# mLSTM stabiliser: the running maximum spread by transfers through HBM and masked on GpSimd, in place of three products a head

## The chip, the cores and the metric

The kernel runs on one core of one Trainium2 chip. The metric is the device time of a run in microseconds (us), as the median of three runs. Five engines are spoken of: TensorE (PE, matrix products), VectorE (DVE), ScalarE (ACT), GpSimd (POOL) and SyncE (SP, which here issues most transfers). Each takes its own instructions strictly in order; they wait for one another by semaphores. PSUM is the memory that products accumulate in, SBUF the one that the engines work from.

## The reference

Two layers of a streaming-encoder trunk for 256 positions and a width of 1024, in float32. Each layer has a token mixer and a gated MLP. In the mixer one input projection feeds a latent attention (MLA, 8 heads) and an mLSTM (8 heads of 64), whose results are projected, merged by gates and projected again. A conditioning vector c gives shifts, scales and gates (adaLN) by a 1024 x 6144 projection per layer.

What the change touches is the mLSTM's stabiliser. In the reference, chunk by chunk:

```python
log_d = jnp.where(causal, b[..., :, None] - b[..., None, :] + ih[..., None, :], -jnp.inf)
log_inter = b + m[..., None]
m_t = jnp.maximum(log_inter, jnp.max(log_d, axis=-1))
w_intra = jnp.exp(log_d - m_t[..., None])
s = jnp.einsum("bthd,bshd->bhts", qc, kc) * w_intra
```

The kernel writes this over the whole sequence. With AA[s] the input gate less the summed log forget gates at position s, and M[t] the running maximum of AA (started at 0), the weight of source s for target t is exp(AA[s] - M[t]) for s <= t and 0 beyond. So each of the 8 heads needs its row M[t] on all 128 partitions (which hold s), and the triangle beyond the diagonal masked out.

## The kernel before

Activations lie transposed, channels on partitions, 256 positions along the free axis. Every float32 product is made of three products in a faster format: weights and activations are split in a high and a low part (`whi`, `wlo`, `hh`, `hl`), and whi x hh, whi x hl and wlo x hh are summed. A weight block of 128 x 1024 is loaded by SP (`raw`), rounded to `whi` by an ACT copy, and DVE subtracts to get `wlo`. DVE also works off the adaLN projection, blocks `ada` of 512 KB loaded by SP into two buffers, as a background task.

The order on the engines is that in which the program emits its instructions. The main line emits units of 4 slots, each with 12 weight products; side tasks (Python generators: heads, gates, norms) go on by one step a slot, at each of their `yield`s. In the mixer the main line runs "fillers", the weight products of other projections, and the heads of both branches run beside them as side tasks: `mlstm_head` and, some slots behind it, the attention head `mla_head`. After heads 1 and 3 no filler follows (PLAIN_HEADS), so heads 1 and 2 start in one slot, and 3 and 4. An attention head makes its scores (`kall`, `qall`), ACT exponentiates them (p), scales them by the inverse sum, PE transposes them (`cst`, the identity, with p), ACT copies them out, and PE multiplies by the values `vv`.

`gates` (line 689 on) makes AA and, by a scan on DVE (line 743), M as an 8 x 256 tile. Before the change ACT rounds M into `mr` rows 0 to 7 and DVE writes the remainder into rows 32 to 39. `mlstm_head` (line 881 on) spreads a row by products: a selector `selr` with ones in the two rows of a head gives M[t] on all partitions in a PSUM bank E (256 columns, then 128 again for the second half of s), and the identity times `maskr` adds the mask of large numbers to the two diagonal blocks. One slot later ACT takes exp(AA - E) from the bank into `dd`; one later DVE multiplies with the query-key products S (`qm`, `km`) to `pw`; one later PE multiplies `pw` with the values `vaug`. Every fourth head goes on with the output of four heads.

`late_constants` (line 1311 on), a side task in the first units, fetches the selector and the mask by two transfers issued on ACT's queue, and ten slots later copies them into `selr` and `maskr` on ACT. POOL adds squares for the norms, takes rsqrt by a power, and issues the transfers that spread the rotary key (`kr` to `kall`); its rows are else empty during the heads. Temporary tiles of one size share a ring of buffers (`w384`: 6 of 128 x 384 numbers), so a new tile waits for the last reader of the one that it takes over. DVE and ACT have a window of 8, so that an emission order differs little from the executed one.

Of the kernel before, what the change touches and what calls it, by code (L numbers as in the profile page):

```python
# [19 lines left out]
P = 128  # L20
T = 256
# [47 lines left out]
NATIVE = 2  # L69
DELAYS = dict(kr=6, c=1, gates=3)  # L70
MLA_DELAY = (3, 2)
LATER = (2, 2, 2, 1)


# [117 lines left out]
def hybrid_trunk(ctx, tc, a):  # L192
# [15 lines left out]
    upool = pool("upool", 1)  # L208
    work = pool("work", 1)
    psum = pool("psum", 1, PSUM)  # L210

    uid = [0]

    def nm(s):
        uid[0] += 1
        return f"{s}_{uid[0]}"

    def bank():
        return psum.tile([P, 512], F32, name=nm("bank"), tag="bank", bufs=8)
# [1 line left out]
    def w256(dt=F32, tag="w256", bufs=8):  # L221
        return work.tile([P, T], dt, name=nm(tag), tag=tag, bufs=bufs)

    def w384(tag="w384", bufs=6):
        return work.tile([P, 384], F32, name=nm(tag), tag=tag, bufs=bufs)

    def w512(tag="w512", bufs=4):
# [375 lines left out]
    def mixer(l, n, begun):  # L603
# [24 lines left out]
        stA, sA = sub("cqkv")  # L628
        gt = sA.tile([40, T], F32, name=nm("gt"), tag="gt")
        ats = sA.tile([8, T], F32, name=nm("ats"), tag="ats")  # L630
        M = sA.tile([8, T], F32, name=nm("M"), tag="M")
        cc_ = sA.tile([P, 5, T], F32, name=nm("cqkv"), tag="cqkv")
        cbank = bank()
        later = LATER if begun else (0,) * 4
# [54 lines left out]
        def gates():  # L689
            b1 = bank()  # L690
            for tb in range(2):
                pe.transpose(b1[:, tb * 40:tb * 40 + 40], gt[:, tb * P:(tb + 1) * P], ident[:40, :40])
            yield
            dve.tensor_copy(gs, b1[:, :80].rearrange("p (b g) -> p b g", b=2))
            iT, fT = gs[:, :, 0:8], gs[:, :, 32:40]

            def g8():
                return work.tile([P, 2, 8], F32, name=nm("g8"), tag="g8", bufs=10)

            ab = g8()  # L700
            dve.scalar_tensor_tensor(ab, fT, -1.0, fT, ALU.mult, ALU.max)
            e = g8()
            act.activation(e, ab, AF.Exp, scale=-1.0)
            yield
            r = g8()
            dve.tensor_scalar(r, e, 2.0, None, ALU.add)
            dve.reciprocal(r, r)
            u = g8()
            dve.tensor_tensor(u, e, r, ALU.mult)
            u2 = g8()  # L710
            dve.tensor_tensor(u2, u, u, ALU.mult)
            p = g8()
            dve.tensor_scalar(p, u2, 1.0 / 17.0, None, ALU.mult)
            for d in (15.0, 13.0, 11.0, 9.0, 7.0, 5.0, 3.0):
                dve.scalar_tensor_tensor(p, p, 1.0 / d, u2, ALU.add, ALU.mult)
            dve.scalar_tensor_tensor(p, p, 1.0, u, ALU.add, ALU.mult)
            mn = g8()
            dve.tensor_scalar(mn, fT, 0.0, None, ALU.min)
            lf = g8()
            dve.scalar_tensor_tensor(lf, p, -2.0, mn, ALU.mult, ALU.add)  # L720
            mg = 1.5 * 2.0 ** 15
            for src, dst in ((lf, LF), (iT, II)):
                dve.tensor_scalar(dst[:, :, 0:8], src, mg, -mg, ALU.add, ALU.add)
                dve.tensor_tensor(dst[:, :, 8:16], src, dst[:, :, 0:8], ALU.subtract)
            for _ in range(6 + later[0]):
                yield
            cs = bank()
            pe.matmul(cs[:, 0:16], tri, LF[:, 0, :], start=True, stop=True)
            pe.matmul(cs[:, 16:32], ones, LF[:, 0, :], start=True, stop=False)
            pe.matmul(cs[:, 16:32], tri, LF[:, 1, :], start=False, stop=True)  # L730
            yield
            dve.tensor_copy(CS, cs[:, 0:32].rearrange("p (b g) -> p b g", b=2))
            dve.tensor_tensor(AA, II, CS, ALU.subtract)
            act.activation(ealo, AA[:, :, 8:16], AF.Exp)
            for _ in range(2 + later[1]):
                yield
            dve.tensor_copy(vaug[:, :, :, 64], ealo)
            at = bank()
            for tb in range(2):
                pe.transpose(at[0:8, tb * P:(tb + 1) * P], AA[:, tb, 0:8], ident)  # L740
            yield
            dve.tensor_copy(ats, at[0:8, :T])
            dve.tensor_tensor_scan(M, ats, ats, 0.0, ALU.max, ALU.max)
            act.copy(mr[0:8], M)
            for _ in range(2 + later[2]):
                yield
            dve.tensor_tensor(mr[32:40], M, mr[0:8].bitcast(F32), ALU.subtract)
            mt_ = bank()
            for tb in range(2):
                pe.transpose(mt_[:, tb * 8:tb * 8 + 8], M[:, tb * P:(tb + 1) * P], ident[:8, :8])  # L750
            yield
            m = g8()
            dve.tensor_tensor(m, mt_[:, 0:16].rearrange("p (b g) -> p b g", b=2), CS[:, :, 0:8], ALU.add)
            dve.tensor_tensor(m, m, CS[:, :, 8:16], ALU.add)
            act.activation(floor, m, AF.Exp, scale=-1.0)
# [123 lines left out]
                                  ALU.subtract)  # L879

        def mlstm_head(hd, nb, spair):
            E = bank()
            sl = selr[:, hd:hd + 1].to_broadcast([40, P])
            pe.matmul(E[:, 0:T], sl, mr, start=True, stop=False)
            pe.matmul(E[:, T:384], sl, mr[:, P:T], start=False, stop=False)
            pe.matmul(v2(E)[:, :, 0:P], identr, maskr.unsqueeze(1).to_broadcast([P, 2, P]), start=False, stop=True)
            if not spair:
                for r0 in (0, 64):
                    spair.append((bank(), qm[hd // 4][r0:r0 + 64, hd // 2 % 2, :],
# [3 lines left out]
                for S, q_, k_ in spair:  # L893
                    pe.matmul(S[:, T:384], k_[:, P:T], q_[:, P:T], start=True, stop=True)
            S = spair[hd % 2][0]
            yield
            dd = w384()
            act.activation(dd[:, 0:T], E[:, 0:T], AF.Exp, scale=-1.0, bias=AA[:, 0, hd:hd + 1])
            act.activation(dd[:, T:384], E[:, T:384], AF.Exp, scale=-1.0, bias=AA[:, 1, hd:hd + 1])
            yield  # L900
            pw = w384()
            dve.scalar_tensor_tensor(pw, S[:, :384], 1.0 / 32.0, dd, ALU.mult, ALU.mult)
# [399 lines left out]
    W.queue_split(W.at)  # L1302
    W.flush()
    pe.window, act.window, dve.window, gp.window = 1000, 8, 8, 1000
    mr = const.tile([40, T], F32R, name="mr")
    gp.memset(mr.bitcast(F32), 0.0)
    selr = const.tile([40, NH], F32R, name="selr")
    identr = const.tile([P, P], F32R, name="identr")
    maskr = const.tile([P, P], F32R, name="maskr")

    def late_constants():
        for _ in range(8):
            yield
        act.copy(identr, ident)
        todo = ((selr, "sel", small(NH)[0:40]), (maskr, "mask", w256()[:, :P]))
        for _, src, t in todo:
            with tc.issue_after(act.done[-1]):
                nc.scalar.dma_start(t, a[src])
        for _ in range(10):
            yield  # L1320
        for dst, _, t in todo:
            act.copy(dst, t)

    setup_stack.close()

# [40 lines left out]
def _constants():  # L1366
# [5 lines left out]
    csts = np.zeros((P, 2), np.float32)  # L1372
    csts[:, 0] = (10000.0 ** (-np.arange(16) / 16.0)).astype(np.float32)[i // 8]
    csts[:, 1] = np.where(i % 32 < 16, -1.0, 1.0)
    sel = np.zeros((40, NH), np.float32)
    for h in range(NH):
        sel[h, h] = 1.0
        sel[32 + h, h] = 1.0
    return cst, mask, csts, sel


def _w_in_columns():
# [22 lines left out]
def _layout(i):  # L1405
# [1 line left out]
    out = {}  # L1407
    out["x"] = np.ascontiguousarray(i["x"][0].T.reshape(KB, P, T).transpose(1, 0, 2))
    out["pos"] = np.tile(i["positions"].astype(np.int32).reshape(8, 32), (16, 1))
    out["cst"], out["mask"], out["csts"], out["sel"] = _constants()  # L1410

    pp = np.zeros((P, DEPTH, NPP), np.float32)

# [57 lines left out]
```

## Time and profile before

| what | us |
|---|---|
| median of 3 runs | 833.68 (833.14 to 833.95) |
| the profiled execution, its own time | 837.23 |
| its span, first to last instruction | 835.4 |
| PE busy in the span | 799.9 (96%) |
| DVE busy | 687.6 (82%) |
| ACT busy | 498.8 (60%) |
| POOL busy | 58.8 (7%) |

The mean granted clock of PE over the span is 0.982 of full. Times of instructions are from the start of the span. In layer 0 the heads run from about 110 to 180 us, in layer 1 from about 505 to 575. Products are pipelined: the time of one in the trace overlaps the next one's, so what a group of products costs PE is read from start to start.

### The profile page before, as it was taken

The numbers are of one execution on the slowest core, as the hardware profiler recorded it, in microseconds if no ns is written. First come the engines' busy times: TensorE is split into PE (matmuls) and PEld (weight loads), VectorE is DVE, ScalarE is ACT, GpSimd is POOL, SyncE is SP. The second block draws the span as 40 slices with busy tenths as digits, with TensorE's granted clock in tenths as the row PEclk, the third lists the DMA queues.
The fourth block names the chain that finished last, engine by engine and source line by source line (L and its number), as shares of the span: only waits on it lengthen the run. The fifth ranks groups of instructions, "written<-read, shape, count | busy, mean of one in ns | idle before, by whom it ended". The sixth has DMA issues, their size and how long they took to land.

```text
span 835.4 us, 16784 instructions
## 1 busy us (share of the span) xinstructions
PE 799.9 (96%) x6496; PEld 781.3 (94%) x6496; DVE 687.6 (82%) x1243; ACT 498.8 (60%) x907; POOL 58.8 (7%) x78
## 2 busy tenths in 40 slices
PE   4879899999999999999999999999999999999995
PEld 3879799999999999999999999899999999999995
DVE  4677898888989998888968987887887998889752
ACT  5267556663558666654548674566455866665551
POOL 3701000000010000000111000000002000000010
PEclk8989999999999999999999999999999999999998
DMA  8967488777674775558985468777755565556841
GB/s 319 360 203 252 142 293 274 246 248 271 218 244 156 256 229 179 163 177 296 347 329 176 133 206 279 241 243 248 270 177 175 167 213 188 178 152 199 287 133 52
DMA packets 56819, 186.25 MB, mean 223 GB/s; under 512 B 6882, under 2 KB 8610, under 8 KB 56738
## 3 DMA queue, kind: packets, MB, share of 16 engines
q1 hardware_dynamic: 56096, 183.98, 66.1%
q0 software_dynamic: 448, 1.11, 0.6%
q8 instruction: 51, 0.84, 0.4%
q14 instruction: 30, 0.25, 0.1%
q10 hardware_dynamic: 194, 0.07, 0.0%
HBM read 182.98 MB, written 1.05 MB: 220 GB/s over the span
## 4 chain that ended last, share of the span: by engine, by line
PE 73%; DVE 10%; DMA 6%; issue 5%; POOL 3%; ACT 2%; DVEq 0%; POOLq 0%; SPq 0%; ACTq 0%
PE bank L183 63%; PE bank L185 11%; DMA ada<-in_ada 5%; DVE wlo L183 3%; POOL rot L183 2%; DVE ada L183 2%; DVE w L183 1%; DVE z L183 1%; DVE hl L183 1%; DMA w<-in_mask 1%; DVE ub L183 1%; DMA kr<-rot 1%; DMA raw<-in_w_down 1%; ACT w L183 0%; ACT whi L183 0%
## 5 line engine op out<-in xcount | busy, mean ns | idle before, releaser
L183 ACT CAST whi<-raw 128x1024 fp32r<-128x1024 f32 (+3 forms) x276 | 261.5, 956 | 125.2 <-PE bank L183 78.8
L183 DVE TENSOR_TENSOR wlo<-raw,whi 128x1024 fp32r<-128x1024 f32 (+3 forms) x276 | 304.9, 1110 | 34.8 <-PE bank L183 14.3
L183 PE MATMUL bank<-hh,whi 128*128 128x256 f32 x980 | 280.9, 287 | 1.3 <-ACT w L183 1.3
L183 PE MATMUL bank<-hh,wlo 128*128 128x256 f32 x981 | 276.3, 282 | 1.1 <-DVE wlo L183 1.1
L183 PE MATMUL bank<-hl,whi 128*128 128x256 f32 x981 | 276.9, 282 | 0.0
L183 PEld LDWEIGHTS bank<-hh,whi 128*128 128x128 f32 x980 | 186.2, 190 | 2.7 <-ACT w L183 1.5
L183 PEld LDWEIGHTS bank<-hh,wlo 128*128 128x128 f32 x981 | 186.3, 190 | 1.5 <-DVE wlo L183 1.5
L183 PEld LDWEIGHTS bank<-hl,whi 128*128 128x128 f32 x981 | 186.6, 190 | 0.9 <-DVE hl L183 0.3
L183 DVE SCALAR_TENSOR_TENSOR ada<-ada,sact 128x1024 f32<-128x1024 f32 x96 | 117.6, 1231 | 13.3 <-DMA ada<-in_ada 13.1
L183 DVE SCALAR_TENSOR_TENSOR z<-bank,pp,z 128x255 f32<-128x255 f32 (+2 forms) x208 | 95.2, 477 | 18.5 <-ACT z L183 16.2
L183 PE MATMUL bank<-gh,wlo 128*128 128x256 f32 x352 | 99.2, 282 | 0.8 <-DVE wlo L183 0.7
L183 PE MATMUL bank<-gl,whi 128*128 128x256 f32 x352 | 99.2, 282 | 0.0
L183 PE MATMUL bank<-gh,whi 128*128 128x256 f32 x352 | 99.0, 281 | 0.0
L183 PEld LDWEIGHTS bank<-gh,wlo 128*128 128x128 f32 x352 | 66.4, 189 | 1.2 <-DVE wlo L183 1.2
L183 PEld LDWEIGHTS bank<-gh,whi 128*128 128x128 f32 x352 | 66.4, 189 | 0.0
L183 PEld LDWEIGHTS bank<-gl,whi 128*128 128x128 f32 x352 | 66.4, 189 | 0.0
L183 PE MATMUL bank<-ub,whi 128*128 128x256 f32 (+1 forms) x256 | 59.2, 282 | 0.0
L183 ACT ACTIVATE z<-bank,pp 128x256 f32<-128x256 f32 x96 | 49.1, 558 | 8.4 <-PE bank L183 4.4
L183 ACT ACTIVATE w<-z 128x256 f32<-128x256 f32 x60 | 25.1, 418 | 36.7 <-DVE z L183 35.3
L183 PEld LDWEIGHTS bank<-ub,whi 128*128 128x128 f32 x256 | 44.0, 189 | 0.0
L185 PE MATMUL bank<-hh,whi 128*128 128x256 f32 x140 | 41.5, 297 | 0.0
L185 PE MATMUL bank<-hh,wlo 128*128 128x256 f32 x139 | 39.1, 282 | 0.0
(259 smaller groups left out, 1371.6 us busy)
## 6 DMA issues: line engine op xcount, KB each, us to landing
ada<-in_ada SPq DMA_DIRECT2D x96, 512.0 KB, 5.1
raw<-in_w_up SPq DMA_DIRECT2D x88, 512.0 KB, 4.4
raw<-in_w_in SPq DMA_DIRECT2D x64, 512.0 KB, 5.3
raw<-in_w_down SPq DMA_DIRECT2D x32, 384.0 KB, 4.2
raw<-in_w_down SPq DMA_DIRECT2D x32, 320.0 KB, 3.7
raw<-in_w_out SPq DMA_DIRECT2D x16, 512.0 KB, 4.8
raw<-in_w_first SPq DMA_DIRECT2D x8, 512.0 KB, 6.5
raw<-in_w_bra SPq DMA_DIRECT2D x8, 512.0 KB, 5.4
```

The lines of the kernel that those rows point to most:

```text
L183: r = f(*args, **kw)
L185: r = f(*args, **kw)
```

## The change

M gets 384 columns: POOL writes its second half of positions again behind the 256, and a transfer on POOL's queue stores the 8 rows in a scratch tile `Mrows` in HBM. Each head fetches its row by one transfer on POOL's queue, repeated to 128 partitions, straight into the tile `dd`; POOL adds the mask `beyond` to the two diagonal blocks in place; three slots later (before: one, after the products) ACT takes the exponential in place. The bank E, its three products, `mr`, `selr`, `identr`, `maskr`, ACT's copies into them, DVE's remainder and the selector input are gone. The mask is fetched straight into `beyond`, issued where it was before on ACT's queue. The ring `w384` has 7 buffers, since `dd` is held longer.

```diff
@@ -69,6 +69,7 @@
 NATIVE = 2
 DELAYS = dict(kr=6, c=1, gates=3)
 MLA_DELAY = (3, 2)
+BROADCAST_SLOTS = 3
 LATER = (2, 2, 2, 1)
 
 
@@ -208,6 +209,7 @@
     upool = pool("upool", 1)
     work = pool("work", 1)
     psum = pool("psum", 1, PSUM)
+    dram = pool("dram", 1, bass.MemoryType.DRAM)
 
     uid = [0]
 
@@ -221,7 +223,7 @@
     def w256(dt=F32, tag="w256", bufs=8):
         return work.tile([P, T], dt, name=nm(tag), tag=tag, bufs=bufs)
 
-    def w384(tag="w384", bufs=6):
+    def w384(tag="w384", bufs=7):
         return work.tile([P, 384], F32, name=nm(tag), tag=tag, bufs=bufs)
 
     def w512(tag="w512", bufs=4):
@@ -628,7 +630,8 @@
         stA, sA = sub("cqkv")
         gt = sA.tile([40, T], F32, name=nm("gt"), tag="gt")
         ats = sA.tile([8, T], F32, name=nm("ats"), tag="ats")
-        M = sA.tile([8, T], F32, name=nm("M"), tag="M")
+        M = sA.tile([8, 384], F32, name=nm("M"), tag="M")
+        Mrows = dram.tile([8, 384], F32, name=nm("Mrows"), tag="Mrows")
         cc_ = sA.tile([P, 5, T], F32, name=nm("cqkv"), tag="cqkv")
         cbank = bank()
         later = LATER if begun else (0,) * 4
@@ -740,11 +743,11 @@
                 pe.transpose(at[0:8, tb * P:(tb + 1) * P], AA[:, tb, 0:8], ident)
             yield
             dve.tensor_copy(ats, at[0:8, :T])
-            dve.tensor_tensor_scan(M, ats, ats, 0.0, ALU.max, ALU.max)
-            act.copy(mr[0:8], M)
+            dve.tensor_tensor_scan(M[:, 0:T], ats, ats, 0.0, ALU.max, ALU.max)
+            gp.tensor_scalar(M[:, T:384], M[:, P:T], 1.0, None, ALU.mult)
+            nc.gpsimd.dma_start(Mrows, M)
             for _ in range(2 + later[2]):
                 yield
-            dve.tensor_tensor(mr[32:40], M, mr[0:8].bitcast(F32), ALU.subtract)
             mt_ = bank()
             for tb in range(2):
                 pe.transpose(mt_[:, tb * 8:tb * 8 + 8], M[:, tb * P:(tb + 1) * P], ident[:8, :8])
@@ -879,11 +882,10 @@
                                   ALU.subtract)
 
         def mlstm_head(hd, nb, spair):
-            E = bank()
-            sl = selr[:, hd:hd + 1].to_broadcast([40, P])
-            pe.matmul(E[:, 0:T], sl, mr, start=True, stop=False)
-            pe.matmul(E[:, T:384], sl, mr[:, P:T], start=False, stop=False)
-            pe.matmul(v2(E)[:, :, 0:P], identr, maskr.unsqueeze(1).to_broadcast([P, 2, P]), start=False, stop=True)
+            dd = w384()
+            nc.gpsimd.dma_start(dd, Mrows[hd:hd + 1, :].to_broadcast([P, 384]))
+            own = dd.rearrange("p (n t) -> p n t", n=3)[:, 0:3:2, :]
+            gp.tensor_tensor(own, own, beyond.unsqueeze(1).to_broadcast([P, 2, P]), ALU.add)
             if not spair:
                 for r0 in (0, 64):
                     spair.append((bank(), qm[hd // 4][r0:r0 + 64, hd // 2 % 2, :],
@@ -893,10 +895,10 @@
                 for S, q_, k_ in spair:
                     pe.matmul(S[:, T:384], k_[:, P:T], q_[:, P:T], start=True, stop=True)
             S = spair[hd % 2][0]
-            yield
-            dd = w384()
-            act.activation(dd[:, 0:T], E[:, 0:T], AF.Exp, scale=-1.0, bias=AA[:, 0, hd:hd + 1])
-            act.activation(dd[:, T:384], E[:, T:384], AF.Exp, scale=-1.0, bias=AA[:, 1, hd:hd + 1])
+            for _ in range(BROADCAST_SLOTS):
+                yield
+            act.activation(dd[:, 0:T], dd[:, 0:T], AF.Exp, scale=-1.0, bias=AA[:, 0, hd:hd + 1])
+            act.activation(dd[:, T:384], dd[:, T:384], AF.Exp, scale=-1.0, bias=AA[:, 1, hd:hd + 1])
             yield
             pw = w384()
             dve.scalar_tensor_tensor(pw, S[:, :384], 1.0 / 32.0, dd, ALU.mult, ALU.mult)
@@ -1302,24 +1304,13 @@
     W.queue_split(W.at)
     W.flush()
     pe.window, act.window, dve.window, gp.window = 1000, 8, 8, 1000
-    mr = const.tile([40, T], F32R, name="mr")
-    gp.memset(mr.bitcast(F32), 0.0)
-    selr = const.tile([40, NH], F32R, name="selr")
-    identr = const.tile([P, P], F32R, name="identr")
-    maskr = const.tile([P, P], F32R, name="maskr")
+    beyond = const.tile([P, P], F32, name="beyond")
 
     def late_constants():
         for _ in range(8):
             yield
-        act.copy(identr, ident)
-        todo = ((selr, "sel", small(NH)[0:40]), (maskr, "mask", w256()[:, :P]))
-        for _, src, t in todo:
-            with tc.issue_after(act.done[-1]):
-                nc.scalar.dma_start(t, a[src])
-        for _ in range(10):
-            yield
-        for dst, _, t in todo:
-            act.copy(dst, t)
+        with tc.issue_after(act.done[-1]):
+            nc.scalar.dma_start(beyond, a["mask"])
 
     setup_stack.close()
 
@@ -1372,11 +1363,7 @@
     csts = np.zeros((P, 2), np.float32)
     csts[:, 0] = (10000.0 ** (-np.arange(16) / 16.0)).astype(np.float32)[i // 8]
     csts[:, 1] = np.where(i % 32 < 16, -1.0, 1.0)
-    sel = np.zeros((40, NH), np.float32)
-    for h in range(NH):
-        sel[h, h] = 1.0
-        sel[32 + h, h] = 1.0
-    return cst, mask, csts, sel
+    return cst, mask, csts
 
 
 def _w_in_columns():
@@ -1407,7 +1394,7 @@
     out = {}
     out["x"] = np.ascontiguousarray(i["x"][0].T.reshape(KB, P, T).transpose(1, 0, 2))
     out["pos"] = np.tile(i["positions"].astype(np.int32).reshape(8, 32), (16, 1))
-    out["cst"], out["mask"], out["csts"], out["sel"] = _constants()
+    out["cst"], out["mask"], out["csts"] = _constants()
 
     pp = np.zeros((P, DEPTH, NPP), np.float32)
```

The line numbers of the program shift by one to three, so rows that stayed differ in those.

On POOL, layer 0, from the second transfer of the rotary key (`kall`) on, these rows stand before (`sm` are powers for norms, the second of them behind mLSTM head 3, `sqs` squares after the heads):

```order
L185 TENSOR_TENSOR sm_749<-sm_747,minus_half 128x4
L666 DMA kall_667<-kr_698 32x8x256
L185 TENSOR_TENSOR sm_1715<-sm_1711,minus_half 128x8
L185 TENSOR_TENSOR sm_2085<-sm_2081,minus_half 128x8
L185 TENSOR_TENSOR sqs_2679<-sq_2677,sq_2682 128x256
```

and these now (`w_228`, `w_243`, `w_244`, `w_273`, `w_274` are the tiles `dd` of heads 0, 1, 2, 3 and 4):

```order
L669 DMA kall_665<-kr_697 32x8x256
L186 TENSOR_SCALAR M_673<-M_673 8x128
L748 DMA Mrows_674<-M_673 8x384
L886 DMA w_228_1291<-Mrows_674 128x384
L186 TENSOR_TENSOR w_228_1291<-w_228_1291,beyond 128x2x128
L886 DMA w_243_1380<-Mrows_674 128x384
L886 DMA w_244_1383<-Mrows_674 128x384
L186 TENSOR_TENSOR w_243_1380<-w_243_1380,beyond 128x2x128
L186 TENSOR_TENSOR w_244_1383<-w_244_1383,beyond 128x2x128
L886 DMA w_273_1509<-Mrows_674 128x384
L886 DMA w_274_1512<-Mrows_674 128x384
L186 TENSOR_TENSOR w_273_1509<-w_273_1509,beyond 128x2x128
```

M's second copy, the write and the heads' transfers and additions have come between; the transfers of heads 1 and 2 stand behind head 0's addition, those of heads 3 and 4 behind the additions of 1 and 2.

On ACT around the mask's transfer, in the first layer's input projection (`z` and `w` belong to the convolution, `qall` to the attention's queries), before:

```order
L183 ACTIVATE w_162_896<-z_815 128x256
L183 ACTIVATE w_163_898<-z_817 128x256
L1318 DMA w_165_914<-in_mask 128x128
L183 CAST whi_1040<-raw_933 128x512
L183 CAST maskr<-w_165_914 128x128
L183 ACTIVATE z_1013<-bank_935,pp 128x256
L183 ACTIVATE z_1015<-bank_935,pp 128x256
L183 CAST whi_1090<-raw_1008 128x1024
L183 ACTIVATE w_175_978<-z_936 128x256
```

and now:

```order
L184 ACTIVATE w_163_895<-z_814 128x256
L184 ACTIVATE w_164_897<-z_816 128x256
L1313 DMA beyond<-in_mask 128x128
L184 CAST whi_1012<-raw_926 128x1024
L184 CAST whi_1035<-raw_928 128x512
L184 ACTIVATE z_1008<-bank_930,pp 128x256
L184 ACTIVATE z_1010<-bank_930,pp 128x256
L184 CAST whi_1085<-raw_1003 128x1024
L184 ACTIVATE w_174_973<-z_931 128x256
```

The transfer has kept its place, and the copy into `maskr`, which stood two rows behind it and ahead of the `z` activations, is gone; `beyond` is read on POOL.

On ACT around head 3 of layer 0, before (`w_287` and `w_288` are `dd` of heads 3 and 4, taken from the banks; `w_274` and `w_285` the attention weights of heads 1 and 2, made from a bank and later scaled in place):

```order
L183 CAST whi_1577<-raw_1383 128x1024
L183 COPY w_273_1517<-bank_1480 128x384
L183 ACTIVATE w_274_1519,sm_1520<-bank_1460,sm_1488 128x128
L183 ACTIVATE w_274_1519,sm_1520<-bank_1460,sm_1488 128x256
L183 ACTIVATE ua_1213<-bank_1385 128x2x256
L183 ACTIVATE w_274_1519<-w_274_1519,sm_1563 128x128
L183 ACTIVATE w_274_1519<-w_274_1519,sm_1563 128x256
L183 ACTIVATE w_285_1567,sm_1568<-bank_1494,sm_1524 128x128
L183 ACTIVATE w_285_1567,sm_1568<-bank_1494,sm_1524 128x256
L183 ACTIVATE w_287_1571<-bank_1528,AA_656 128x256
L183 ACTIVATE w_287_1571<-bank_1528,AA_656 128x128
L183 ACTIVATE w_288_1574<-bank_1532,AA_656 128x256
```

and now (`w_273` is `dd` of head 3; `w_269` and `w_281` the attention weights of heads 1 and 2, `w_267` a copy of transposed ones):

```order
L184 COPY w_267_1494<-bank_1459 128x384
L184 CAST whi_1556<-raw_1369 128x1024
L184 ACTIVATE w_269_1498,sm_1499<-bank_1441,sm_1466 128x128
L184 ACTIVATE w_269_1498,sm_1499<-bank_1441,sm_1466 128x256
L184 ACTIVATE ua_1206<-bank_1371 128x2x256
L184 ACTIVATE w_273_1509<-w_273_1509,AA_654 128x256
L184 ACTIVATE w_281_1552,sm_1553<-bank_1471,sm_1505 128x128
L184 ACTIVATE w_269_1498<-w_269_1498,sm_1545 128x128
L184 ACTIVATE w_269_1498<-w_269_1498,sm_1545 128x256
L184 ACTIVATE w_281_1552,sm_1553<-bank_1471,sm_1505 128x256
L184 ACTIVATE w_273_1509<-w_273_1509,AA_654 128x128
L184 ACTIVATE w_274_1512<-w_274_1512,AA_654 128x256
```

The first exponential of head 3 has moved ahead of the scaling of attention head 1; before, it stood behind it.

## Rows read from the trace of the kernel before

**Rows 1.** busy time by stretch: us, busy us (instructions) per engine, granted clock, DMA share, GB/s

```profile
110.00:180.00 70.00, 70.00 (x565) 65.75 (x563) 58.84 (x125) 43.94 (x105) 3.29 (x2) 1.00 0.81 264
...
505.00:575.00 70.00, 68.69 (x538) 64.17 (x537) 54.46 (x119) 41.12 (x100) 3.29 (x2) 0.98 0.76 254
```

**Rows 2.** what PE waited for, 60 to 110: total us, times, longest

```profile
PE bank L185 <- DVE wlo L183: 2.4, 1, 2.4
```

**Rows 3.** timeline of ACT, 86 to 94: start, us, instruction, [idle before, releaser]

```profile
86.72 0.37 ACTq L1318 DMA_DIRECT2D w<-in_mask  x1
88.42 0.62 ACT L183 CAST whi<-raw 128x512 fp32r<-128x512 f32 x1 [1.30 <-PE bank L185]
92.50 0.30 ACT L183 CAST maskr<-w 128x128 fp32r<-128x128 f32 x1 [3.45 <-DMA w<-in_mask]
92.70 1.01 ACT L183 ACTIVATE z<-bank,pp 128x256 f32<-128x256 f32 x2
```

**Rows 4.** transfers: issues, KB each, median us to landing

```profile
w<-in_mask ACTq DMA_DIRECT2D x1, 64.0 KB, 5.8
```

**Rows 5.** timeline of PE, 94 to 97.5

```profile
96.86 0.39 PE L185 MATMUL bank<-ua,wlo 128*128 128x256 f32 x1 [2.38 <-DVE wlo L183]
```

**Rows 6.** the two stretches of slow clock (columns as rows 1)

```profile
98.00:102.00 4.00, 3.63 (x20) 3.38 (x19) 3.88 (x9) 1.64 (x5) 0.00 (x0) 0.57 0.37 123
532.00:536.00 4.00, 3.79 (x20) 3.79 (x21) 2.88 (x6) 3.02 (x9) 0.00 (x0) 0.58 0.89 337
```

**Rows 7.** timeline of PE at head 0 and at heads 1 and 2

```profile
114.27 0.44 PE L185 MATMUL bank<-mr,selr 40*128 40x256 f32 x2
...
114.96 0.49 PE L185 MATMUL bank<-qm,km 64*128 64x256 f32 x2
...
123.02 0.44 PE L185 MATMUL bank<-mr,selr 40*128 40x256 f32 x2
...
124.39 0.49 PE L185 MATMUL bank<-qm,km 64*128 64x256 f32 x2
```

**Rows 8.** timeline of DVE: the scan, and head 0's product with its weights

```profile
105.58 0.68 DVE L183 TENSOR_TENSOR_SCAN M<-ats 8x256 f32<-8x256 f32 x1
...
117.80 0.55 DVE L183 SCALAR_TENSOR_TENSOR w<-bank,w 128x384 f32<-128x384 f32 x1
```

**Rows 9.** timeline of ACT: head 0's exponentials

```profile
115.26 0.73 ACT L183 ACTIVATE w<-bank,AA 128x256 f32<-128x256 f32 x2
```

**Rows 10.** the rotary key's tile kr, loads on POOL's queue, 16 KB each

```profile
DMA to landing us min/median/max: 3.3/5.0/5.8
```

**Rows 11.** the tile kall, transfers on POOL's queue: ns min/median/max; landing

```profile
L666 POOL DMA_DIRECT2D kall<-kr x4: 583/613/634, 69.3 to 455.4; - x4
...
DMA to landing us min/median/max: 3.3/4.6/5.8
```

**Rows 12.** the tile sqs, POOL's additions: ns min/median/max

```profile
L185 POOL TENSOR_TENSOR sqs<-sqs,sq x20: 733/768/2529, 227.7 to 818.7; 128x256 f32<-128x256 f32 x20
```

**Rows 13.** timeline of PE, attention's transposes in the heads' stretch

```profile
130.23 0.49 PE L185 MATMUL bank<-cst,w 128*128 128x128 f32 x3
...
139.28 0.49 PE L185 MATMUL bank<-cst,w 128*128 128x128 f32 x3
```

**Rows 14.** timeline of DVE, the same instruction beside an addition on POOL and without

```profile
232.65 0.95 DVE L183 SCALAR_TENSOR_TENSOR ub<-x,am,ua 128x256 fp32r<-128x256 f32 x1
...
634.06 0.49 DVE L183 SCALAR_TENSOR_TENSOR ub<-x,am,ua 128x256 fp32r<-128x256 f32 x1 [0.58 <-ACT ua L183]
```

**Rows 15.** timeline of POOL, that addition

```profile
232.52 0.80 POOL L185 TENSOR_TENSOR sqs<-sqs,sq 128x256 f32<-128x256 f32 x1 [4.03 <-ACT sq L183]
```

**Rows 16.** what PE waited for, 505 to 575

```profile
PE bank L183 <- ACT w L183: 1.3, 1, 1.3
```

**Rows 17.** what DVE waited for, 505 to 575

```profile
DVE ada L183 <- DMA ada<-in_ada: 6.9, 5, 2.9
```

**Rows 18.** the chain behind PE's wait, 505 to 545: start, us, what

```profile
517.40 7.71 DMA ada<-in_ada
```

## The prediction

> **What bounds the kernel now.** I read the busy time by stretches first. In the two stretches where the mLSTM heads run, TensorE (PE) is busy 70.00 of 70 us in layer 0 and 68.69 of 70 in layer 1, VectorE (DVE) 58.84 and 54.46, ScalarE (ACT) 43.94 and 41.12, GpSimd (POOL) only 3.29, and the DMA engines 0.81 and 0.76 [rows 1]. So PE sets the time there, and every product taken out of its row shortens the run, unless something that now hides behind those products comes late. Then the waits of PE. Just ahead of the layer-0 heads its longest is 2.4 us, for a weight remainder `wlo` of DVE [rows 2], and following it back by ACT's timeline ends at a transfer that this change moves: the copy of the mask (`maskr`) stands 3.45 us for in_mask, which was issued at 86.72 and takes 5.8 us to land [rows 3, 4]. Behind it in ACT's queue stand the `z` activations at 92.70, DVE needs them before the `wlo` that PE awaits, and PE starts again at 96.86 after 2.38 us [rows 5]. After that gap the clock is granted at 0.57 of full over the 4 us from 98, part of it at the lower of its two levels, 1.2 in place of 2.4 GHz [rows 6].
>
> **Products removed.** Head 0's three products hold PE from 114.27 until the query-key product starts at 114.96: 0.69 us. For heads 1 and 2, which start together, it is 123.02 to 124.39: 1.37 for two [rows 7]. 16 heads in two layers at 0.685 make 10.9 us. PE was never idle there, so the whole of it lies on the path: -10.9. The scan that makes M ends at 106.26, so these products waited for nothing.
>
> **Mask wait removed.** The mask now goes straight into a constant that only POOL reads, so ACT's row loses the copy and its wait. The activations at 92.70 could have run about 2.7 us earlier (ACT was free at 89.04, and 88.42 + 0.62 is the copy before). PE's 2.38 goes, and with it the slow clock behind: 4 us at 0.57 lost 4 x 0.43 = 1.7 [rows 5, 6]. Bounds: 0 if another weight is late in its place, -4.1 if not. DVE's own idle time there was for the same activations, so I take -4.1.
>
> **Broadcasts added, on POOL and its queue.** A head now needs a transfer of 128 x 384 numbers, 196,608 bytes, from scratch in HBM, then a GpSimd addition on 128 x 256 elements, then ACT's exponential. The nearest transfer is kall from kr, 256 KB on the same queue: 0.61 us to issue, 3.3, 4.6 or 5.8 us (shortest, median, longest) to landing [rows 11]. The nearest addition is the 128 x 256 of the squares: 0.73 to 2.53, median 0.77 [rows 12]. The row write to HBM is nearest to kr from rot, 16 KB: median 5.0 [rows 10]. The bytes are no matter: 1.57 MB a layer beside some 18.5 MB in that stretch (70 us at 264 GB/s [rows 1]) raise the DMA share from 0.81 to about 0.88.
>
> The Trainium skill, page "DMA: Bandwidth & Descriptors", section "Anatomy of one DMA — SWDGE (gpsimd) path", fits a GpSimd-issued DMA as 2.0 us plus bytes at 436 GB/s. By it this broadcast would land in about 2.45 us (an estimate from that page), kall's in 2.6; the trace has no kall under 3.3, so under this traffic it disagrees, and by it the sum would be that of the first rival.
>
> Start of layer 0: M is there at 106.26 [rows 8]; 0.6 for the duplicating copy, 0.6 + 5.0 for the write, 0.6 + 4.6 + 0.8 for head 0 brings its weights' argument at about 118.5, against an exponential at 115.26 and DVE's product with it at 117.80 before [rows 8, 9]. The products that need it stand two slots later now, so about 3 us later: no wait, in the middle. Heads 1 and 2 are issued behind head 0's addition on POOL: landing at about 123.7, their additions end at 125.3, exponentials follow, where ACT had theirs at 123.8. ACT's scaling of the first attention head queues behind them. With the longest landings this becomes 2.8 us late. Bounds 0 and +2.8; I take the half, +1.4.
>
> Head 3: its tile is one that head 0's attention weights fill until PE has transposed them (130.23, 0.33 us of starts [rows 13]). From 130.6 it needs 0.6 to issue, L to land, 0.8 to add, 1.5 for its exponential and for the scaling of attention head 1 behind it in ACT's row: 2.9 + L. PE wants that head's transposes at 139.28, or 137.9 without the 1.37 of products between [rows 7, 13]: a budget of 7.3. At L = 4.6 it is 0.2 late, at 5.8 it is 1.4, at 3.3 not at all. Heads 5, 6 and 7 have over 10 us. Beside it PE has new short waits, where a product now stands close behind ACT's copy of transposed weights, without the three products as cover. Per layer +0.75 for both (bounds 0 and +2.5): +1.5.
>
> POOL's additions may also slow DVE. At 232.52 an addition of 0.80 us ran [rows 15], and DVE's `ub` from 232.65 took 0.95 us where such a one takes 0.49 [rows 14]: 0.46 more. All 16 so: 7.4 us of DVE, 3.7 a layer, against 11.2 idle in layer 0's stretch [rows 1]. Cover, so 0 in layer 0; in layer 1 it is within the next term.
>
> The Trainium skill, page "SBUF — State Buffer", section "Who interferes with whom", says that a DVE instruction with two SBUF inputs and a GpSimd one that reads SBUF share one read interface, and the later of them is held up for the whole of the other. The stretched pair above agrees. By that rule the DVE time above could lie on the path, which is the second rival.
>
> Layer 1: it is not PE alone that bounds. PE waits 1.3 us there for ACT [rows 16], followed by 4 us at 0.58 of the clock [rows 6]; the chain behind goes back to an ada transfer of 7.71 us at 517.40 [rows 18], and DVE stands 6.9 us for such [rows 17]. PE arrives earlier, the transfers don't: of the 5.5 us of heads I take 2.3 as lost (bounds 0 and 5.5; two heads of three before that wait are worth 2.06).
>
> **Sum.** -10.9 - 4.1 + 1.4 + 1.5 + 2.3 = -9.8. The profiled execution (837.23, span 835.4) would become 827.4; it lies 3.5 above the median of the runs, 833.68, which I take as base: 823.9, said as 824.
>
> **Rivals.** *All of it hidden.* POOL has 66 us idle, and heads 0 to 2 of layer 1 can be fetched some 20 us ahead. Then -15.0, and if the filler bank of layer 1 no longer waits, its 1.3 and the 1.7 of slow clock go too: -18.0, that is 816 to 819. Against: landings of 4.6 with head 3's budget of 7.3.
> *Supply of weights and ada blocks bounds.* DVE at 84% and DMA at 81% are near enough [rows 1]; the products then only filled time in which those arrived, and the additions stretch DVE. What is left is the mask's 4.1: 829.6. Against: PE had no wait at all in layer 0's stretch.
> *Slower: the transfers land late.* One mechanism: each head's weights hang on an HBM transfer in a busy stretch, and POOL, which waits in order for each landing, issues the next only then. At the 7.7 us that the long ada transfer took, 3.1 over kall's median, the first heads of layer 0 come 6.2 late (head 0's and head 1's landings in a row), head 3 of either layer 3.3, the later heads 0.3 a layer: 13.4; three of these gaps are long enough for the slow clock, 3 x 1.7 = 5.1; with 2.3 and 1.2 from above 22.0 come back against 15.0: +7.0, 840.7. It decides from a landing of about 6.1 (4 x 1.5 + 0.4 + 5.1 + 3.5 = 15.0). For it: the layer's transfers peak here. Against: no kall took over 5.8.
>
> **Chances.** Forecast 0.55, its own range 819 to 830; all hidden 0.15; supply 0.13; slower 0.15; other 0.02. The range 816 to 835 holds the first three and the near edge of the fourth. Below 0.2%, or 1.7 us, a measurement of this kernel tells nothing from no change: faster 0.79, same 0.06 (from the supply case and the edge), slower 0.15.
>
> **What would show it.** Layer 0's wait of 2.38 at 96.86 and the slow clock behind it gone; query-key products directly behind weight products; POOL's transfers landing in 4 to 5 us; short PE waits on ACT at heads 1 to 4, none over 1.5; DVE still idle for ada near 522. It is wrong if PE waits over 2 us in the heads' stretches with a slow clock behind, if the landings exceed 6 us, or if the wait at 96.86 has another cause in its place.

## The result: slower by 1.28%

| | median, us | before beside it | ratio (95% interval) |
|---|---|---|---|
| changed kernel | 844.74 (842.61 to 846.49) | 833.41 | 1.0128 (1.0101 to 1.0154) |

The forecast was 824.0, from 816 to 835. The time is 11.3 us over before, on the side of the rival that had the transfers land late. The profiled execution of the changed kernel took 845.15 us (span 843.3); the one of before that the prediction was read from took 837.23, 3.8 above the median of its runs, so the two traces differ by less (7.9) than the medians.

The two stretches of the heads, in the columns of [rows 1]:

```profile
110.00:180.00 70.00, 61.75 (x446) 56.33 (x446) 49.60 (x105) 36.77 (x89) 17.75 (x17) 0.93 0.78 252
...
505.00:575.00 70.00, 66.74 (x520) 61.48 (x520) 57.84 (x111) 42.93 (x95) 13.40 (x13) 1.00 0.80 261
```

In layer 0 every engine but POOL does less in the same 70 us. The largest gap stands at 107 to 126 us; an experiment below shows what it is worth. First POOL's timeline, with M's copy, the write, head 0's transfer and its addition:

```profile
103.28 2.55 POOL L186 TENSOR_SCALAR M<-M 8x128 f32<-8x128 f32 x1 [32.24 <-DVE M L184]
106.13 0.58 POOL L748 DMA_DIRECT2D Mrows<-M  x1 [0.29 <-POOL M L186]
111.48 0.61 POOL L886 DMA_DIRECT2D w<-Mrows  x1 [4.77 <-DMA raw<-in_w_in]
118.33 0.71 POOL L186 TENSOR_TENSOR w<-w,beyond 128x256 f32<-128x256 f32 x1 [6.24 <-DMA w<-Mrows]
```

The 4.77 us before head 0's transfer are the wait for the write of M, which landed 5.07 us after its issue, at 111.20; the row names a weight load, but in the kernel without additions (below) the same wait is put down to that write. Then ACT's timeline, where head 0's exponential (`w<-w,AA`) is the next thing in the row:

```profile
106.99 0.23 ACT L184 ACTIVATE floor<-g 128x16 f32<-128x16 f32 x1
119.08 0.51 ACT L184 ACTIVATE w<-w,AA 128x256 f32<-128x256 f32 x1 [11.87 <-POOL w L186]
119.50 1.03 ACT L184 CAST whi<-raw 128x1024 fp32r<-128x1024 f32 x1
```

Then DVE's, which needs the `whi` copied at 119.50:

```profile
111.34 0.75 DVE L184 TENSOR_TENSOR vaug<-bank,ealo 128x256 f32<-128x256 f32 x2
120.56 1.22 DVE L184 TENSOR_TENSOR wlo<-raw,whi 128x1024 fp32r<-128x1024 f32 x1 [8.48 <-ACT whi L184]
121.70 1.22 DVE L184 SCALAR_TENSOR_TENSOR ada<-ada,sact 128x1024 f32<-128x1024 f32 x1
...
122.85 1.74 DVE L184 SCALAR_TENSOR_TENSOR ada<-ada,sact 128x1024 f32<-128x1024 f32 x1
...
124.52 0.55 DVE L184 SCALAR_TENSOR_TENSOR w<-bank,w 128x384 f32<-128x384 f32 x1
```

And PE's, which reaches head 0's values:

```profile
120.39 0.28 PE L186 MATMUL bank<-hh,wlo 128*128 128x256 f32 x1
125.12 1.55 PE L186 MATMUL bank<-vaug,w 128*128 128x65 f32 x6 [4.46 <-DVE w L184]
```

Read from the top: the row lands 6.8 us after its issue. ACT stands 11.87 us at the exponential. Behind it waits one weight copy. DVE's next instruction needs that copy, so DVE stands 8.48, and when it goes on, a remainder and two ada blocks are in front of head 0's product; so PE loses 4.46 although the row had been there since 118.3. As behind the gap in [rows 5, 6], the granted clock is low afterwards; here are the next 20 us, the granted clock in the third column from the end:

```profile
125.00:130.00 5.00, 4.88 (x22) 4.79 (x23) 4.94 (x11) 1.89 (x7) 0.17 (x1) 0.50 0.84 257
130.00:135.00 5.00, 5.00 (x33) 4.67 (x31) 2.12 (x8) 3.71 (x8) 0.55 (x1) 0.82 1.00 371
135.00:140.00 5.00, 3.58 (x22) 3.03 (x21) 4.98 (x11) 0.81 (x3) 1.60 (x2) 0.86 0.81 265
140.00:145.00 5.00, 4.66 (x30) 4.14 (x28) 3.08 (x8) 1.91 (x8) 3.76 (x2) 0.80 0.85 258
```

0.50 is the lower level, 1.2 GHz; over the four rows at most 5 x (0.50 + 0.18 + 0.14 + 0.20) = 5.1 us of full-speed time were lost, less for what PE stood idle in them. The sixteen row transfers and the two writes of M, in the form of [rows 11]:

```profile
DMA to landing us min/median/max: 3.5/4.9/6.8
```

**A ledger of PE** for the stretch from the transposes of M to the first product behind the heads (`mh`), made from the trace by adding up the time from each product's start to the next one's, with recorded idle time apart. "Before" is a second profiled execution of that kernel (below), "head 0 in turn" and "constant" are experiments.

| layer 0, us | before | after | head 0 in turn | constant |
|---|---|---|---|---|
| the products removed | 5.3 | 0 | 0 | 0 |
| idle | 0.2 | 8.3 | 5.7 | 2.0 |
| weight products | 83.7 | 88.8 | 87.0 | 85.5 |
| other products | 19.4 | 22.4 | 20.9 | 19.3 |
| stretch | 108.6 | 119.4 | 113.5 | 106.8 |
| **layer 1, us** | | | | |
| the products removed | 5.3 | 0 | 0 | 0 |
| idle | 1.2 | 3.6 | 3.6 | 2.1 |
| weight products | 105.0 | 107.5 | 107.4 | 106.7 |
| other products | 19.4 | 20.5 | 20.1 | 19.4 |
| stretch | 130.9 | 131.6 | 131.1 | 128.2 |

The products cost what the prediction said, 10.6 us in all. Layer 0 takes 10.8 longer all the same, and layer 1, whose first three rows are fetched 20 us ahead, 0.7 longer. Each column is one execution. Three executions with all heads by products (two of before, one with the mask copied later) have 108.3, 108.6 and 109.7 us in layer 0, but 132.9, 130.9 and 129.6 in layer 1. So layer 0's loss stands far outside of what executions differ by, and the 0.7 of layer 1 does not.

### The profile page after: what moved, and what is told of

Same layout as the page of the kernel before. It is cut to its first block, busy times and chain, and to the rows that moved or that the text cites. A ratio compares the mean times of both kernels' runs of the same rounds, so it can differ in the third digit from the quotient of the medians.

```text
span 843.3 us, 16715 instructions
## 1 busy us (share of the span) xinstructions
PE 798.3 (95%) x6448; PEld 777.0 (92%) x6448; DVE 690.3 (82%) x1241; ACT 498.0 (59%) x902; POOL 94.0 (11%) x113
## 5 line engine op out<-in xcount | busy, mean ns | idle before, releaser
L184 PE MATMUL bank<-hh,wlo 128*128 128x256 f32 x974 | 273.9, 282 | 1.1 <-DVE wlo L184 1.1
L184 PE MATMUL bank<-hl,whi 128*128 128x256 f32 x974 | 274.0, 282 | 0.0
L184 PEld LDWEIGHTS bank<-hh,whi 128*128 128x128 f32 x974 | 184.1, 189 | 1.5 <-issue 0.3
L184 PEld LDWEIGHTS bank<-hh,wlo 128*128 128x128 f32 x974 | 183.9, 189 | 1.6 <-DVE wlo L184 1.5
L184 PEld LDWEIGHTS bank<-hl,whi 128*128 128x128 f32 x974 | 184.2, 189 | 0.8 <-DVE hl L184 0.4
L184 DVE SCALAR_TENSOR_TENSOR ada<-ada,sact 128x1024 f32<-128x1024 f32 x96 | 118.9, 1244 | 19.9 <-DMA ada<-in_ada 19.4
L186 POOL TENSOR_TENSOR sqs<-sq,sq 128x256 f32<-128x256 f32 x4 | 3.3, 826 | 368.0 <-issue 281.4
```

Of the source, the lines that this page charges most:

```text
L184: r = f(*args, **kw)
L186: r = f(*args, **kw)
```

## The experiments

**Before, once more.** The unchanged kernel, for its trace.

> The kernel before, unchanged, for a second profiled execution. Theory (the mask wait of 2.4 us belongs to every run, and what varies from run to run lies in the weight-bound stretch from 370 to 425 us): the wait is there again, and the stretch differs by 1 to 4 us. Rival: no such wait this time.

One run, 836.8. The mask wait of [rows 3] is not there. ACT's timeline around the copy, and the transfer:

```profile
88.60 0.62 ACT L183 CAST whi<-raw 128x512 fp32r<-128x512 f32 x1 [1.28 <-PE bank L185]
89.94 0.30 ACT L183 CAST maskr<-w 128x128 fp32r<-128x128 f32 x1 [0.72 <-DMA w<-in_mask]
90.20 1.02 ACT L183 ACTIVATE z<-bank,pp 128x256 f32<-128x256 f32 x2
```

```profile
w<-in_mask ACTq DMA_DIRECT2D x1, 64.0 KB, 3.0
```

It landed in 3.0 us in place of the 5.8 of [rows 4]. So the 2.38 of PE in [rows 5] does not belong to every execution. The rival was right. The weight-bound stretch from 378 to 421 us, with nothing changed in it, took 5.0 us more this time, measured between the same two `wlo` of DVE; so part of what traces differ by is no work of a change.

**The mask wait alone.**

```diff
+MASK_COPY = 18
...
-        for _ in range(10):
+        for _ in range(MASK_COPY):
             yield
         for dst, _, t in todo:
             act.copy(dst, t)
```

> The kernel before, with the copies of selector and mask on ScalarE eighteen slots behind their transfers in place of ten; heads by products as before. Theory (the mask wait of 2.4 us and the 1.7 of slow clock behind it belong to every run): 829 to 830. Rival (the profiled execution of before, 3.8 above the median, is the one that had them): 832 to 834.

834.50 against 833.26, ratio 1.0008 (0.9981 to 1.0036): nothing that can be told from no change. The interval leaves room for a gain of 1.6 us at most, so the mask term of 4.1 is not there in ordinary runs.

**A constant in place of the rows.** What the change could give if nothing had to be fetched.

```diff
-            nc.gpsimd.dma_start(dd, Mrows[hd:hd + 1, :].to_broadcast([P, 384]))
-            gp.tensor_tensor(own, own, beyond..., ALU.add)
...
-            act.activation(dd[:, 0:T], dd[:, 0:T], AF.Exp, scale=-1.0, bias=AA[:, 0, hd:hd + 1])
+            act.activation(v2(dd[:, 0:T]), beyond..., AF.Exp, scale=-1.0, bias=ealo[:, 0, hd:hd + 1])
```

> The changed kernel without the sixteen row transfers and additions: the exponentials read a constant tile (the weights are not those of the reference). Theory: all that the change gives without its waits, 10.9 of products and the mask's share: 818 to 823. Rival (the products only filled time in which weights and ada blocks arrived): 829 to 833.

829.28 against 833.26, ratio 0.9957 (0.9929 to 0.9984): 4.0 us faster, not 11 to 15. The rival's number holds. In the ledger 10.6 us of products go, 2.6 us of idle come (4.1 against 1.5 over both layers) and 3.5 us of weight products. Of the idle, the longest in layer 0 is at the transposes of the mLSTM's output. The rival's reason, supply, is not shown: DVE stands for ada blocks 5.5 us from 110 to 180 us, but in the second execution of before it stood 5.0 there (in the first 0.7), with all heads by products. The first row is PE's; the second and third are from DVE's waits with a constant and in the second execution of before (total us, times, longest):

```profile
178.84 0.33 PE L184 MATMUL bank<-cst,w 128*128 128x128 f32 x1 [1.20 <-DVE w L184]
```

```profile
DVE ada L184 <- DMA ada<-in_ada: 5.5, 8, 1.8
```

```profile
DVE ada L183 <- DMA ada<-in_ada: 5.0, 6, 1.3
```

The weight products are slower without any idle time or slow clock (granted 1.00 from 104 to 210 us): where a head's products break into their row, the next weight product starts late. PE's timeline of this kernel, weight products 0.12 us apart but for the first behind the values, which holds PE 0.20:

```profile
120.77 0.28 PE L186 MATMUL bank<-hl,whi 128*128 128x256 f32 x1
120.89 0.28 PE L186 MATMUL bank<-hh,wlo 128*128 128x256 f32 x1
121.00 0.78 PE L186 MATMUL bank<-vaug,w 128*128 128x65 f32 x6
121.59 0.36 PE L186 MATMUL bank<-hh,whi 128*128 128x256 f32 x1
121.79 0.28 PE L186 MATMUL bank<-hl,whi 128*128 128x256 f32 x1
121.91 0.28 PE L186 MATMUL bank<-hh,wlo 128*128 128x256 f32 x1
```

Steps of 0.145 us and more from a weight product to what follows, idle time apart: 28 in layer 0's stretch before, 45 here, worth 3.6 and 5.5 us over the ordinary step. The difference of 1.8 us is the whole rise of layer 0's weight products in the ledger. Before, the heads' products came in fewer and longer groups.

**The same with one slot.** BROADCAST_SLOTS = 1 in the kernel with a constant.

> The kernel with a constant in place of transfers and additions, with one slot ahead of the exponential as before the change in place of three (the weights are not those of the reference). Theory (with three slots the heads' products break into the weight products at some 18 more places in layer 0, 0.1 us each): 824 to 828. Rival (the slots cost nothing): 829 to 831.

827.95 against 833.34, ratio 0.9942 (0.9927 to 0.9957). That is inside the theory's range. The broken steps fall from 45 to 34 and the weight products of layer 0 from 85.5 to 84.5 us, but idle time rises from 2.0 to 2.9, and the kernel is not clearly faster than the one with three slots: the two intervals overlap. Its longest wait of layer 0 is the output chain of four heads, first POOL, then DVE, then PE:

```profile
171.76 2.54 POOL L186 TENSOR_TENSOR sm<-sm,minus_half 128x8 f32<-128x8 f32 x1 [22.89 <-DVE sm L184]
```

```profile
174.34 0.17 DVE L184 TENSOR_TENSOR sm<-sm,sm 128x8 f32<-128x8 f32 x1 [1.53 <-POOL sm L186]
```

```profile
176.40 0.41 PE L186 MATMUL bank<-cst,w 128*128 128x128 f32 x2 [1.32 <-DVE w L184]
```

In the two executions of before PE has no such wait in layer 0.

**Head 0's exponential in its turn.** One position in ACT's row.

```diff
+            held, act.window = act.window, IN_TURN if (l, hd) == (0, 0) else act.window
             act.activation(dd[:, 0:T], dd[:, 0:T], AF.Exp, ...)
             act.activation(dd[:, T:384], dd[:, T:384], AF.Exp, ...)
+            act.window = held
```

(IN_TURN is 0: the instruction keeps its place behind all that was emitted before it.)

> The changed kernel with one thing different: the exponential of head 0 in layer 0 alone is held to its turn, behind one weight copy; all other heads as in the changed kernel. Theory (that copy behind the waiting exponential is the loss): VectorE's 8.5 us of waiting go, layer 0 gives back 5 to 7 of its 11 us, layer 1 stays as in the changed kernel; 836 to 840. Rival (the kernel with all heads in turn gained in its later heads): 842 or more.

838.74 against 833.34, ratio 1.0073 (1.0057 to 1.0089), as expected: by the ratios 4.6 us of the loss are gone, by the medians 6.0, and the interval lies clear of the changed kernel's (1.0101 to 1.0154). In the two traces the order on ACT differs in this one copy alone, and DVE, PE and POOL execute the same instructions in the same order. The row comes no earlier than in the changed kernel (its addition starts at 119.16, there at 118.33); ACT still stands for it, but the copy that DVE needs next is no longer behind:

```profile
119.92 0.81 ACT L185 ACTIVATE w<-w,AA 128x256 f32<-128x256 f32 x2 [9.27 <-POOL w L187]
```

```profile
120.81 0.56 DVE L185 SCALAR_TENSOR_TENSOR w<-bank,w 128x384 f32<-128x384 f32 x1 [3.56 <-ACT w L185]
```

```profile
121.42 0.88 PE L187 MATMUL bank<-vaug,w 128*128 128x65 f32 x6 [0.51 <-DVE w L185]
...
129.47 1.09 PE L187 MATMUL bank<-cst,w 128*128 128x128 f32 x3 [2.60 <-ACT w L185]
```

PE's 4.46 is 0.51. The longest wait that is left looks like the same thing one head further on: head 1's exponential waits for its row until 126.18 in front of the attention's first exponential and scaling, and PE waits 2.60 for these:

```profile
126.18 0.51 ACT L185 ACTIVATE w<-w,AA 128x256 f32<-128x256 f32 x1 [3.57 <-POOL w L187]
126.59 0.35 ACT L185 ACTIVATE w<-bank,sm 128x128 f32<-128x128 f32 x1
...
129.01 0.80 ACT L185 ACTIVATE w<-w,sm 128x128 f32<-128x128 f32 x2 [0.37 <-DVE sm L185]
```

This was not tested apart. In the kernel with M earlier (below) the first three rows land in time, and PE still waits 1.27 us at these transposes, so not all of the 2.60 can be put down to the row.

**All exponentials in turn.** The same lines for every head.

> The changed kernel, with each head's exponential held to its turn in ScalarE's row, behind the weight copy that the changed kernel puts behind it. Theory (layer 0's loss is ScalarE standing at head 0's exponential with that copy behind it, so that VectorE and then TensorE run dry): VectorE's 8.5 us of waiting for the copy go, TensorE's wait of 4.5 at head 0's values shrinks to under 1.5; 835 to 840. Rival (the row itself comes too late for TensorE, whatever stands behind): 843 or more.

839.49 against 834.14, ratio 1.0059 (1.0026 to 1.0092), as expected; layer 0's stretch is 113.1, like the last. Layer 1's is 135.3 us in place of 131.6, in an execution that took 843.20, 3.7 over the median of its runs; there are waits such as this one, at the last output chain:

```profile
584.83 0.69 PE L185 MATMUL bank<-cst,w 128*128 128x128 f32 x2 [2.40 <-DVE w L185]
```

**In turn, and M earlier in layer 0.**

```diff
-DELAYS = dict(kr=6, c=1, gates=3)
+DELAYS = dict(kr=6, c=1, gates=1)
-LATER = (2, 2, 2, 1)
+LATER = (0, 0, 6, 1)
```

> As the last, and in layer 0 the running maximum is made some six slots earlier. Theory: head 0's row lands before its turn, no wait of over 1 us at heads 0 to 2 of layer 0; 831 to 836, near the kernel with a constant (829) and three heads by products (837). Rival (transfers and additions themselves cost): no better than 838.

843.53 against 834.14, ratio 1.0104 (1.0066 to 1.0142): a miss. Rows 0 to 2 do land before their turn, the first at about 104:

```profile
95.69 0.56 POOL L187 TENSOR_SCALAR M<-M 8x128 f32<-8x128 f32 x1 [24.02 <-DVE M L185]
...
104.31 1.65 POOL L187 TENSOR_TENSOR w<-w,beyond 128x256 f32<-128x256 f32 x1 [3.08 <-DMA w<-Mrows]
```

But the gates that were pulled forward cost PE 3.41 us at their transposes, ahead of the heads:

```profile
91.59 0.38 PE L187 MATMUL bank<-cst,AA 128*8 128x128 f32 x2 [3.41 <-DVE AA L185]
```

and four waits of 1.3 to 2.2 us remain in the heads, on the attention's weights and the output chain. The edit moved the gates as well as the rows, so it does not tell what early rows alone would be worth.

**Heads 0 to 2 of layer 0, or all of layer 0, by products.**

```diff
+PRODUCT = {(0, h) for h in range(3)}      # or range(8)
...
+            if (l, hd) in PRODUCT:
+                ... the three products into E, as before ...
+            else:
+                E = dd = w384()
+                nc.gpsimd.dma_start(dd, Mrows[hd:hd + 1, :].to_broadcast([P, 384]))
...
```

Both kernels are made from before, with the selector and mask copied eighteen slots behind their transfers, as in the run on the mask alone.

> Heads 0, 1 and 2 of layer 0 by products, the other thirteen by transfers and additions; six buffers in the ring. Theory (layer 0's start): the wait of 4.5 us at the values of head 0 and the slow clock behind go, the eleven us of layer 0 shrink to 0 to 3: 826 to 833. Rival (transfers and additions cost everywhere): 13 of 16 of the loss stays, 841 or more.

> Layer 0's heads by products as before, layer 1's by transfers and additions; the mask is copied eighteen slots behind its transfer; six buffers in the ring. Theory (the loss is layer 0's start, where head 0's exponential waits for its row in front of a weight copy on ScalarE): no wait of the heads in layer 0, layer 1 gains 1 to 3 us, the mask's share comes on top: 827 to 832. Rival (transfers and additions slow VectorE and the loads in both layers alike): half of the 11.3 stays, 838 or more.

Three heads: 837.07 against 833.26, ratio 1.0032 (1.0009 to 1.0054). So with thirteen of sixteen heads still fetched, 7.7 us of the 11.3 are gone, and layer 0's stretch is 109.8 in place of 119.4: most of the loss was the start of layer 0, not transfers as such. The time missed the theory's 826 to 833 and did not reach below before. All of layer 0 by products: 838.04, ratio 1.0050 (1.0023 to 1.0077). That is the rival's number, not the theory's 827 to 832, and its trace does not settle why. The profiled execution took 842.05, the slowest of ten. In it layer 0, with the same products in the same order on PE as in the run on the mask alone, took 111.6 us against 108.3 to 109.7, and layer 1 134.3 against 129.6 to 132.9 in the executions with all heads by products (133.0 in the kernel with three). In this kernel, what PE waited for from 505 to 600:

```profile
PE bank L185 <- ACT w L185: 4.1, 3, 2.4
PE bank L185 <- DVE w L185: 1.6, 2, 1.2
```

Both kernels have six buffers in the ring in place of seven; how much of this is the ring was not tried apart.

**No additions.**

```diff
-            gp.tensor_tensor(own, own, beyond..., ALU.add)
...
```

> The changed kernel without the sixteen additions of the mask on GpSimd; the exponential takes another bias of the same shape (the weights are not those of the reference). Theory (the additions end with the landings, and only head 0's chain counts): 0.7 us less at head 0, 841 to 845. Rival (additions and VectorE hold each other up): 839 or less.

842.51 against 834.14, ratio 1.0085 (1.0054 to 1.0117): by the medians 2.2 us better than the changed kernel and in the theory's range, though the two intervals overlap. Layer 0's stretch is as long as with additions, 119.4 us. Head 0's exponential starts 0.80 us earlier, at 118.28, with the weight copy still behind it, and PE's wait at head 0's values falls by as much, from 4.46 to 3.66:

```profile
124.09 0.44 PE L186 MATMUL bank<-vaug,w 128*128 128x65 f32 x2 [3.66 <-DVE w L184]
```

No kernel that computes the reference beat before; the kernels with a constant show that this order of instructions would give 4.0 to 5.4 us if all rows came for nothing.

## Why the prediction was wrong

**Start of layer 0, the step that failed.** The prediction had 0 to +2.8, taken as +1.4, for "no wait, in the middle". What came was a wait of 4.46 us with a slow clock behind it, and a stretch 10.8 us longer. The first two of the prediction's own signs of being wrong showed: a wait of over 2 us in the heads with a slow clock behind, and a landing over 6 us. Two things were wrong in the step.

First the durations: M's copy on POOL took 2.55 in place of 0.6, and head 0's landing 6.8 in place of at most 5.8. From the end of the scan to the end of head 0's addition the prediction had 12.2 us, and it took 15.9 (103.19 to 119.04). (The landing times count from the start of the issue, so the 0.6 for each issue was in them already; without that the forecast would have been 11.0.) The clock time, 119.0 against 118.5 foreseen, agrees only by luck, because M was ready 3.1 us earlier in this execution.

Second, the price of a late row: the prediction asked when PE would want head 0's product. It looked at what queues behind the exponentials of heads 1 and 2 on ACT, but not at what stands behind head 0's. A weight copy stood there, in the order of the changed kernel, and DVE's whole row hung on it. Moving that one copy ahead of the exponential took back 4.6 to 6.0 of the 11.3 us, with the row no earlier.

The two faults needed each other. With the order changed and the row still late, PE's wait is 0.51. With the order kept and the row as early as forecast, it would be about 0.8: an estimate, 4.46 less the 3.7 us of lateness, since PE's wait fell by 0.80 with the exponential 0.80 earlier. What the other 5 to 7 us of the loss are made of is shown only in part: three heads by products take 7.7 back, and the waits at head 1 and at the attention's weights were not tried apart.

**The rival that came true** ("each head's weights hang on an HBM transfer") had the place in layer 0 and 7.0 of the 11.3 us. Its condition, landings of over 6.1, held for two rows of sixteen, 6.8 for head 0 and 6.7 for head 5 of layer 0 (the median was 4.9); the mechanism that decides, the order on ACT, it left out.

**The mask's 4.1** was read from one execution whose transfer took 5.8 us; in the second it took 3.0, and with the wait taken away the time is the same within 1.6 us. The prediction saw that its profiled execution stood 3.5 above the median and subtracted a whole term from the median nevertheless.

**The products' 10.9** measured 10.6 of PE's time. But PE 70.00 of 70 busy did not mean that all of it would be given back: with all sixteen row transfers gone, the gain is 4.0 to 5.4. The rest became waits of PE (2.6 us, the longest at the output chain) and 3.5 us of more broken rows of weight products, which the sum had not at all. The rival on supply gave 829.6 for the whole change, which is the time of the kernel with a constant, 829.28; that is luck, since it came from the mask's 4.1 with the products worth nothing, and the mask gave nothing.

**Head 3 and the small waits, +1.5,** were too small: in layer 1, where the start has slack, the transfers cost 131.6 less 128.2, 3.4 us, against the 0.75 a layer of the forecast; these are single executions, but no kernel with rows fetched in layer 1 had less than 130.8 us there, and the two with a constant 128.2 and 127.6. **Layer 1's +2.3** cannot be judged: its stretch before came out anywhere from 129.6 to 132.9. GpSimd's additions were left small, and at 2.2 us, with intervals that overlap, nothing here speaks against it.

**The rules of the Trainium skill.** The estimate of 2.45 us for a row, by the fit in the Trainium skill, "DMA: Bandwidth & Descriptors", section "Anatomy of one DMA — SWDGE (gpsimd) path", is under every landing here (3.5 to 6.8). The rule of the Trainium skill, "SBUF — State Buffer", section "Who interferes with whom", agrees with the traces: M's copy of 0.56 us, when it started ahead of a `wlo` (the kernel with M earlier), took 2.55 beside two of them in the changed kernel. The prediction cited it for the additions, where it mattered little, and not for that copy, which stands on the chain.

## What to carry to other kernels

When a wait is put on an in-order engine, price what is queued behind the waiting instruction, and who needs that, before asking when the waiting result is due; a copy for another consumer behind it can cost more than the late result. A gap of one profiled execution that hangs on one transfer's landing is not a term until a second execution shows it. And a bound engine's busy time is not the gain of removing its work: look for the next chain that the work covered.

## What was not expected of the hardware

Products of another kind in a row of weight products cost PE 0.1 to 0.2 us at each break, beside their own time (steps of 0.20 to 0.31 in place of 0.12), so a head's products that stand apart cost more than the same ones together: 45 breaks in place of 28 are 1.8 us in layer 0 of the kernel with a constant. A 64 KB transfer on the same queue at the same point of the program landed in 5.8 and in 3.0 us in two executions of one kernel. And an 8 x 128 copy on GpSimd took 0.56 us or 2.55 to 2.90, the longer ones beside DVE subtractions.
